# Moving the key half of the second memory projection from differential attention into the first mixing layer

## The chip, the cores and the metric

The kernel runs on one core of one Trainium2 chip. The metric is device microseconds from the first to the last instruction of one execution. TensorE is called PE, VectorE DVE, ScalarE ACT, GpSimd POOL, and SP is SyncE, the engine whose queue issues the loads.

## The reference

A block of two layers over 256 positions of width 1024, followed by a second block of two layers that the change doesn't touch. Each of the first block's layers mixes along the sequence (layer 0: an RWKV-7 recurrence on one half of the width and an S5 state space on the other; layer 1: differential attention), then attends to a memory of 256 rows, which is the same in both layers, then runs a feed-forward part (layer 1: 8 experts). Cut to what matters:

```python
for l in range(DEPTH):
    hn = rms_norm(h, norm_mix[l])
    if l % 2 == 0:
        z = hn @ hy_w_in[i]
        y_a = rwkv7_time_mix(z[..., :RWKV_COLS], ...)
        y_b = s5_ssm(z[..., RWKV_COLS:], ...)          # ends in a gelu and a gated product, the glu
        y_mix = jnp.concatenate([y_a, y_b], axis=-1) @ hy_w_out[i]
    else:
        y_mix = diff_attention(hn, da_w_qkv[i], ...)
    h = h + y_mix
    h = h + memory_cross_attention(rms_norm(h, norm_xattn[l]), rms_norm(mem, norm_mem[l]), ...)
    ...

def memory_cross_attention(h, mem_n, w_q, w_kv, q_gain, k_gain, w_o):
    k, v = jnp.split(mem_n @ w_kv, 2, axis=-1)
    k = rms_norm(k.reshape(b, m, MEM_HEADS, MEM_HEAD_DIM), k_gain)
    ...
```

Keys and values of the memory, `mem_n @ w_kv`, depend on nothing that a layer computes, so they can be made at any earlier time.

## The kernel before

All of it is one program, in stages one after the other: `mix0` (layer 0's mixing), `xa0` (its attention to the memory), `ff0`, `mix1` (differential attention), `xa1`, `ff1` (the experts), then the second block. Products run in a split form: a weight tile is loaded as `raw` (128x1024, 512 KB), ACT rounds it into `whi` (L270), DVE subtracts to get `wlo` (L271), and `mm3` issues three matmuls for each product (L320 to L322). `mix0` has 3 buffers of `raw` and 2 each of `whi` and `wlo`; the other stages have 6 of each.

`mem_kv(l)` is a generator that makes the memory's keys `kT` and values `v` of layer l. It loads the memory (two DMAs), normalizes and transposes it (`norm_T`: 16 transposes L385, 16 splits each on ACT L361 and on DVE L362, squares L401), then goes through four column groups c: 0 and 1 are the keys, 2 and 3 the values. A group is two weight tiles of two halves, with 12 matmuls of 512 columns to each half. A key group is then copied (kn, L548), its heads' squares are summed (L569), an rsqrt is made of them (L348 to L353), the heads are scaled (L519), transposed on PE (L522) and copied to `kT` (L524). A value group is only copied (L544).

Where this work stands in the program is set by hand: `drive(*gens, bg, slow, every)` steps through generators in turn, and each `yield` is a place where others may put their instructions. Each engine then takes its instructions in the order in which they were written, and waits on semaphores. In `mix0`, four recurrence units `mat(0..3)` are driven with the S5 part as `slow` and `mem_kv(0)` behind the rest of the input projections as `bg`; behind them come the glu (product with `yh`, `yl`, matmuls into `psB`) and the output projection. In `mix1`, `attn(0)` has the second half of the qkv projection as its background, `attn(1)` the whole of `mem_kv(1)`, in the order `KV_ORD[1]` = (0, 2, 1, 3); then follows `out_proj`. In `attn`, probabilities p are transposed (L734) and copied (`at`, L739), multiplied by the values (L741 to L743), the outputs copied (`on`, L749), squared (L751), reduced (L752), scaled by an rsqrt (L758), transposed (L761) and split into `oTh` and `oTl`.

Of the kernel before, what the change touches and what calls it, by code (L numbers as in the profile page):

```python
# [9 lines left out]
F32 = mybir.dt.float32  # L10
# [32 lines left out]
ZN = 2  # L43
EI = 2
SE = 2
SG = 1
# [158 lines left out]
def build(tc, dram, off, out, phases):  # L205
# [98 lines left out]
    def every_n(g, n):  # L304
        i = 0
        for _ in g:
            i += 1
            if i % n == 0:
                yield

    def idle(n):
        for _ in range(n):
            yield

    def chain(*fns):
        for f in fns:
            yield from f
# [177 lines left out]
            down_acc(y, lambda k: xh[:, k], lambda k: xl[:, k], name, i, order[0], -1)  # L495
        down_last(y, lambda k: xh[:, k], lambda k: xl[:, k], name, order[last:])

    mem_state, mem_pools, mem_ctx = {}, {}, {}

    def mem_kv(l, tag, st, xp=None):  # L500
        m = [wp.tile([128, 1024], F32, tag="raw", name="mem", bufs=nraw) for _ in range(2)] if rawc == 1024 else None
        if m is None:
            m2 = wp.tile([128, 2, 1024], F32, tag="raw", name="mem", bufs=nraw)
            m = [m2[:, t] for t in range(2)]
        for t in range(2):
            nc.sync.dma_start(m[t], dram("mem")[:, t])
        xh, xl, rm = norm_T(m, "norm_mem%d" % l, tag, xp)
        gk = ap.tile([128, 2], F32, tag="gk", name="gk", bufs=1)
        V.scalar_tensor_tensor(gk, colr("xa_q_gain%d" % l), 1.0 / 16.0, colr("xa_k_gain%d" % l),
                               op0=ALU.mult, op1=ALU.mult)  # L510
        p = mem_pools[l]
        kT, v = p.tile([128, 8, 256], F32, name="kT"), p.tile([128, 2, 1024], F32, name="v")
        mem_state[l] = (kT, v)
        yield
        def heads_T(c, kn, ks):
            for t in range(2):
                for a in range(2):
                    s = slice(a * 256, a * 256 + 256)
                    V.tensor_scalar(kn[t][:, s], kn[t][:, s], ks[t][:, a:a + 1], None, op0=ALU.mult)  # L519
                pt = psC((128, 4, 128))  # L520
                for b in range(4):
                    T.transpose(pt[:, b], kn[t][:, b * 128:(b + 1) * 128], ident)  # L522
                for b in range(2):
                    S.activation(kT[:, 4 * c + b:4 * c + 4:2, t * 128:t * 128 + 128], pt[:, b::2], AF.Copy,  # L524
                                 scale=gk[:, b:b + 1])

        pend = None
        for c in KV_ORD[l]:
            ps = [psA(tag=tag) for _ in range(2)]
            for j in range(2):  # L530
                w = wt("w_kv%d" % l, 2 * c + j)
                for kk in range(4):
                    k = 4 * j + kk
                    for t in range(2):
                        ts = slice(t * 128, t * 128 + 128)
                        wh, wl = w(kk * 512, 512)
                        mm3(ps[t], xh[:, k, ts], xl[:, k, ts], wh, wl, k == 0, k == 7)
                    yield
                if pend:
                    heads_T(*pend)  # L540
                    pend = None
            if c >= 2:
                for t in range(2):
                    S.activation(v[:, t, (c - 2) * 512:(c - 1) * 512], ps[t], AF.Copy, scale=rm[t])  # L544
                continue
            kn = [st.tile([128, 512], F32, tag="kn", name="kn", bufs=2) for _ in range(2)]
            for t in range(2):
                S.copy(kn[t], ps[t])  # L548
            pend = (c, kn, head_norm(kn, rm, 2, 256, st))
        if pend:  # L550
            heads_T(*pend)

    def open_kv(l):
        mem_ctx[l] = ExitStack()
        mem_pools[l] = mem_ctx[l].enter_context(
            tc.tile_pool(name="kv%d" % l, bufs=1, side="right", reuse_waits="tile"))

    def head_norm(src, rm, nh, d, st=None):
        ss = ap.tile([128, 2, nh], F32, tag="hn%d" % nh, name="hn", bufs=2)
# [14 lines left out]
        return [z[:, t] for t in range(2)]  # L574

    def xattn(l):
        kT, v = mem_state[l]
        xh, xl, rm = norm_T(ht, "norm_xattn%d" % l)
        oh = ap.tile([128, 8, 256], F32R, tag="oTh", name="oTh", bufs=1)
        ol = ap.tile([128, 8, 256], F32R, tag="oTl", name="oTl", bufs=1)  # L580
# [57 lines left out]
    def diff_attn():  # L638
# [135 lines left out]
            pass  # L774
        tags[0] = "D"
        pace = None
        open_kv(1)
        kv = mem_kv(1, "D", ap, ap)
        next(kv)
        bg = qkv(1)  # L780
        drive(paced(attn(0)), bg=every(bg, R0))
# [194 lines left out]
    def mix0():  # L976
        nonlocal junk_at
        with tc.tile_pool(name="z", bufs=1, reuse_waits="tile") as zp:
            rrow = zp.tile([128, 256], F32, name="rrow")
            yab = zp.tile([128, 8, 256], F32, tag="yab", name="yab", bufs=1)  # L980
            uT = zp.tile([128, 4, 256], F32, name="uT")
            def zpair(i):
                w = wt("w_z", i)
                for b in range(2):
                    n = ZB[2 * i + b]
                    if n == "Z":
                        continue
                    ps = psA((128, 256), "A")
                    for k in range(8):
                        mm3(ps, *w((b * 8 + k) * 128, 128), xh[:, k], xl[:, k], k == 0, k == 7)  # L990
                        if k == 3:
                            yield None
                    yield n, ps

            with tc.tile_pool(name="rw", bufs=1, reuse_waits="tile") as rp:
                open_kv(0)
                zx, s5x = ExitStack(), ExitStack()
                zxp = zx.enter_context(tc.tile_pool(name="zx", bufs=1, side="right", reuse_waits="tile"))
                junk_at = (zxp, 512)
                xh, xl, rm = norm_T(ht, "norm_mix0", xp=zxp)  # L1000
                bcast_row(rm, zp, rrow)
                with tc.tile_pool(name="s5prep", bufs=1, reuse_waits="tile") as sp:
                    s5c = s5_prep(zp, sp)

                def s5():
                    zx.close()
                    sp = s5x.enter_context(tc.tile_pool(name="s5", bufs=1, side="right", reuse_waits="tile"))
                    yield from s5_table(sp, s5c)
                    yield from s5_main(sp, s5c, yab, uT)

                rwkv(rp, zpair, yab, uT, rrow, s5())
                s5x.close()
            with tc.tile_pool(name="mo", bufs=1, reuse_waits="tile") as sp:
                junk_at = (sp, 512)
                s5_glu(sp, s5c, yab)
                mh = sp.tile([128, 8, 256], F32R, name="mh")
                ml = sp.tile([128, 8, 256], F32R, name="ml")
                for k in range(8):
                    split(mh[:, k], ml[:, k], yab[:, k])
                out_proj(mh, ml, "w_hyo", LM)  # L1020
                junk_at = None

    def rwkv(rp, zpair, ya, uT, rrow, s5g):
# [26 lines left out]
        def t2(name, shape, n=2):  # L1050
            return mp.tile(list(shape), F32, tag=name, name=name, bufs=n)
# [32 lines left out]
        zg = zgen()  # L1084
        nonlocal junk_at
        junk_at = (rp, 256)
        kv = mem_kv(0, "D", rp)
        mctx = ExitStack()

        def need(n):  # L1090
# [82 lines left out]
        def mat(p):  # L1173
# [47 lines left out]
            for j in range(5):  # L1221
# [17 lines left out]
                V.tensor_tensor(TN[:, lo:], TZ[:, lo:], pT[:, lo:], op=ALU.subtract)  # L1239
                TZ = TN  # L1240
                yield
            PQ = t2("PQ", (128, 4, 2, 64))
            pq = psB((128, 4, 128))
            heads(lambda c, g: T.matmul(pq[g, c], TZ[g, 1, c], X[g, c].rearrange("p a t -> p (a t)"), start=True, stop=True))
            S.mul(PQ.rearrange("p c a t -> p (c a t)"), pq.rearrange("p c t -> p (c t)"), -1.0)
            yield
            MT = t2("MT", (128, 4, 64))
            HT = t2("HT", (128, 4, 64))
            pm = psC((128, 4, 2, 64))
            heads(lambda c, g: T.matmul(pm[g, c, 0], PQ[g, c, 0], VB[g, c, 1], start=True, stop=True))  # L1250
# [23 lines left out]
            ms = t2("ms", (128, 8))  # L1274
            V.tensor_reduce(ms[:, :4], po, axis=AX, op=ALU.add)
            V.tensor_scalar(ms[:, :4], ms[:, :4], 1.0 / 64, None, op0=ALU.mult)
            ct = t2("ct", (128, 4, 64))
            V.tensor_tensor(ct, po, ms[:, :4, None].to_broadcast([128, 4, 64]), op=ALU.subtract)
            yield
            cq = e("cq", (128, 4, 64))  # L1280
# [24 lines left out]
        def zrest():  # L1305
            for _ in zg:
                yield
# [2 lines left out]
        drive(ew(0), ew(1))  # L1310
        next(kv)
        mp = mctx.enter_context(tc.tile_pool(name="mat", bufs=1, reuse_waits="tile"))
        drive(chain(mat(0), mat(2)), chain(idle(SG), mat(1), mat(3)), chain(ew(2), ew(3)),
              bg=chain(every_n(zrest(), ZN), kv), slow=slow, every=SE)
        drive(kv)
        drive(slow)
        mctx.close()

# [433 lines left out]
    for pi, ph in enumerate(phases):  # L1752
# [13 lines left out]
        with tc.tile_pool(name=ph, bufs=1, reuse_waits="tile") as ap:  # L1766
            if ph == "mix0":
                mix0()
            elif ph in ("xa0", "xa1"):
                l = int(ph[2])  # L1770
                if l not in mem_state:
                    open_kv(l)
                    drive(mem_kv(l, "D", ap, ap))
                xattn(l)
                mem_ctx[l].close()
            elif ph == "mix1":
                diff_attn()
            elif ph == "ff0":
                ffn(None)
            elif ph == "ff1":  # L1780
                moe()
                rq = None
            elif ph in ("b0", "b1"):
                block2(int(ph[1]))
            elif ph in ("bf0", "bf1"):
                ffn(int(ph[2]))
# [36 lines left out]
```

## Time and profile before

| | us |
|---|---|
| time, median of 3 runs (lowest, highest) | 2551.97 (2551.45, 2552.53) |
| the profiled execution: its span | 2550.7 |
| PE busy | 2437.5 (96%) |
| DVE busy | 2050.5 (80%) |
| ACT busy | 1501.3 (59%) |
| mean granted TensorE clock | 0.965 |

The profiled execution's own time is its span, 2550.7 us; the median of the timed runs lies 1.3 us above it. Busy shares are means over all stages; what a stage is limited by is read from stretches of it. A clock of 1.00 is 2.4 GHz and 0.50 is 1.2 GHz. In the timelines a row with a count stands for that many instructions one after the other, and a bracket gives the idle time before the row and the instruction that ended it.

### The profile page before, as it was taken

Reading aid. Unit: us, or ns where it says so; the run is one execution under the profiler, and the core shown is the slowest. Engines: PE = TensorE matmul, PEld = TensorE weight load, DVE = VectorE, ACT = ScalarE, POOL = GpSimd, SP = SyncE. Lnnn points to the kernel's source line nnn. Section 1 sums busy time; section 2 is a strip of 40 time slices with the busy share of each in tenths; the row PEclk is TensorE's granted clock in tenths of the full one; section 3 lists DMA queues with packets and bytes.
Section 4 is the critical chain, followed back from the end, with each engine's and each line's share of the span. In section 5 each row is a group of like instructions: output and inputs, shape, how many; then the busy total and the mean of one; then the engine's idle time right before and its main releaser. Section 6 shows DMA issues by size and latency. Waiting matters only on the chain. (4 is left out here: it accounts for less than half of the span.)

```text
span 2550.7 us, 38313 instructions
## 1 busy us (share of the span) xinstructions
PE 2437.5 (96%) x13843; PEld 2009.8 (79%) x13843; DVE 2050.5 (80%) x3526; ACT 1501.3 (59%) x2236; POOL 115.3 (5%) x144
## 2 busy tenths in 40 slices
PE   7979878999999989999999999999998999999999
PEld 6856657899777778787878787878786689976998
DVE  8696866666766569999999999998987778876886
ACT  6321225544656557777777777777775455564654
POOL 2341300000000000000000000000000000000000
PEclk9986979999999989999999999999998899998999
DMA  5310115455534559999998999999994355552553
GB/s 183 103 43 25 51 58 189 157 184 188 169 108 141 190 178 373 357 330 356 357 357 324 362 357 326 361 326 366 348 356 152 100 167 189 184 182 76 185 186 107
DMA packets 154756, 558.12 MB, mean 219 GB/s; under 512 B 17568, under 2 KB 18208, under 8 KB 154560
## 3 DMA queue, kind: packets, MB, share of 16 engines
q1 hardware_dynamic: 152064, 551.62, 61.2%
q10 hardware_dynamic: 2496, 3.99, 0.5%
q8 instruction: 110, 1.80, 0.3%
q14 instruction: 86, 0.70, 0.1%
HBM read 554.50 MB, written 1.05 MB: 218 GB/s over the span
## 5 line engine op out<-in xcount | busy, mean ns | idle before, releaser
L271 DVE TENSOR_TENSOR wlo<-raw,whi 128x1024 fp32r<-128x1024 f32 x1044 | 1254.2, 1227 | 208.9 <-ACT whi L270 195.8
L270 ACT CAST whi<-raw 128x1024 fp32r<-128x1024 f32 x1044 | 1074.6, 1050 | 553.6 <-PE psA L322 249.2
L321 PE MATMUL psB<-wlo,xeh 128*128 128x512 f32 x880 | 351.3, 399 | 3.3 <-DVE wlo L271 3.3
L322 PE MATMUL psB<-whi,xel 128*128 128x512 f32 x880 | 348.0, 395 | 0.0
L320 PE MATMUL psB<-whi,xeh 128*128 128x512 f32 x880 | 345.4, 396 | 0.1
L321 PE MATMUL psB<-xTl,whi 128*128 128x256 f32 x1008 | 283.7, 282 | 0.0
L320 PE MATMUL psB<-xTh,whi 128*128 128x256 f32 x1008 | 281.8, 283 | 1.5 <-DVE fg L1734 1.5
L322 PE MATMUL psB<-xTh,wlo 128*128 128x256 f32 x1008 | 282.4, 281 | 0.0
L321 PEld LDWEIGHTS psB<-wlo,xeh 128*128 128x128 f32 x880 | 165.2, 188 | 48.0 <-DVE wlo L271 9.6
L320 PEld LDWEIGHTS psB<-whi,xeh 128*128 128x128 f32 x880 | 165.3, 188 | 39.8 <-ACT whi L270 1.0
L322 PEld LDWEIGHTS psB<-whi,xel 128*128 128x128 f32 x880 | 165.3, 188 | 37.8
L322 PEld LDWEIGHTS psB<-xTh,wlo 128*128 128x128 f32 x1008 | 191.0, 190 | 0.4
L321 PEld LDWEIGHTS psB<-xTl,whi 128*128 128x128 f32 x1008 | 189.6, 188 | 1.1
L320 PEld LDWEIGHTS psB<-xTh,whi 128*128 128x128 f32 x1008 | 187.5, 187 | 3.2 <-DVE fg L1734 2.1
L320 PE MATMUL psA<-whi,xTh 128*128 128x512 f32 x416 | 171.8, 421 | 4.8 <-ACT whi L270 4.6
L321 PE MATMUL psA<-wlo,mhh 128*128 128x512 f32 x448 | 175.8, 394 | 0.2
L322 PE MATMUL psA<-whi,mhl 128*128 128x512 f32 x448 | 173.9, 392 | 1.2 <-DVE mhl L359 1.2
L321 PE MATMUL psA<-wlo,xTh 128*128 128x512 f32 x416 | 169.9, 412 | 0.5 <-DVE wlo L271 0.5
L322 PE MATMUL psA<-whi,xTl 128*128 128x512 f32 x416 | 164.1, 409 | 0.0
L320 PE MATMUL psA<-whi,mhh 128*128 128x512 f32 x448 | 152.5, 392 | 1.7 <-ACT mhh L358 1.7
L320 PE MATMUL psA<-whi,hh 128*128 128x512 f32 x264 | 103.3, 391 | 1.5 <-ACT hh L358 1.5
L321 PE MATMUL psA<-wlo,hh 128*128 128x512 f32 x264 | 103.2, 391 | 0.0
(570 smaller groups left out, 3882.3 us busy)
## 6 DMA issues: line engine op xcount, KB each, us to landing
raw<-in_w_moe SPq DMA_DIRECT2D x672, 512.0 KB, 6.1
raw<-in_w_bfu SPq DMA_DIRECT2D x88, 512.0 KB, 4.2
raw<-in_w_ffu SPq DMA_DIRECT2D x44, 512.0 KB, 4.5
raw<-in_w_bfd SPq DMA_DIRECT2D x44, 512.0 KB, 4.1
raw<-in_w_kv SPq DMA_DIRECT2D x32, 512.0 KB, 3.6
raw<-in_w_in SPq DMA_DIRECT2D x32, 512.0 KB, 5.4
raw<-in_w_qkv SPq DMA_DIRECT2D x24, 512.0 KB, 4.5
raw<-in_w_ffd SPq DMA_DIRECT2D x22, 512.0 KB, 4.5
```

Source lines behind the costliest of these rows:

```text
L270: S.copy(hi, raw[:, r])
L271: V.tensor_tensor(lo, raw[:, r], hi.bitcast(F32), op=ALU.subtract)
L320: T.matmul(ps, ah, bh, start=st, stop=False)
L321: T.matmul(ps, ah, bl, start=False, stop=False)
L322: T.matmul(ps, al, bh, start=False, stop=sp)
```

## The change

The keys of layer 1 are made in `mix0`, behind those of layer 0: `mem_kv` takes an `order` of column groups, and `chain(mem_kv(0), mem_kv(1, order=(0, 1)))` is the background of the recurrence. What is left of the background when the recurrence units are done is written out by `drive(bg)`. In `mix1`, `mem_kv(1)` runs with groups (2, 3) alone; it loads and normalizes the memory as it did, so the normalization for layer 1 is done in both places. The pool of keys and values of a layer is opened in two parts, and the keys' part for layer 1 lives from `mix0` on. To make room, `PQ` shares the buffers of `TZ`, `MT` those of `Y` and `ct` those of `HT` in the recurrence units.

```diff
-    def mem_kv(l, tag, st, xp=None):
+    def mem_kv(l, tag, st, xp=None, order=None):
+        order = order or KV_ORD[l]
...
-        p = mem_pools[l]
-        kT, v = p.tile([128, 8, 256], F32, name="kT"), p.tile([128, 2, 1024], F32, name="v")
-        mem_state[l] = (kT, v)
+        kT, v = mem_state.get((l, "k")), mem_state.get((l, "v"))
...
-        for c in KV_ORD[l]:
+        for c in order:
...
-    def open_kv(l):
-        mem_ctx[l] = ExitStack()
-        mem_pools[l] = mem_ctx[l].enter_context(
-            tc.tile_pool(name="kv%d" % l, bufs=1, side="right", reuse_waits="tile"))
+    def open_kv(l, part):
+        mem_ctx.setdefault(l, ExitStack())
+        p = mem_ctx[l].enter_context(
+            tc.tile_pool(name="kv%d%s" % (l, part), bufs=1, side="right", reuse_waits="tile"))
+        mem_state[l, part] = p.tile([128, 8, 256] if part == "k" else [128, 2, 1024], F32, name="kT" if part == "k" else "v")
...
-        open_kv(1)
-        kv = mem_kv(1, "D", ap, ap)
+        open_kv(1, "v")
+        kv = mem_kv(1, "D", ap, ap, (2, 3))
...
-                open_kv(0)
+                open_kv(1, "k")
+                open_kv(0, "k")
+                open_kv(0, "v")
...
-        kv = mem_kv(0, "D", rp)
+        kv = chain(mem_kv(0, "D", rp), mem_kv(1, "D", rp, order=(0, 1)))
...
-            PQ = t2("PQ", (128, 4, 2, 64))
+            PQ = t2("TZ", (128, 4, 2, 64), 4)
...
-            MT = t2("MT", (128, 4, 64))
+            MT = t2("Y", (128, 4, 64))
...
-            ct = t2("ct", (128, 4, 64))
+            ct = t2("HT", (128, 4, 64))
...
-        drive(chain(mat(0), mat(2)), chain(idle(SG), mat(1), mat(3)), chain(ew(2), ew(3)),
-              bg=chain(every_n(zrest(), ZN), kv), slow=slow, every=SE)
-        drive(kv)
+        bg = chain(every_n(zrest(), ZN), kv)
+        drive(chain(mat(0), mat(2)), chain(idle(SG), mat(1), mat(3)), chain(ew(2), ew(3)), bg=bg, slow=slow, every=SE)
+        drive(bg)
         drive(slow)
```

What this does to the order of instructions is shown at three places. Lines of the changed kernel are a few lower or higher than those of before (L521 there is L522 here, L1297 and L1298 are L1295 and L1296).

First, PE at the end of `mix0`: `zG` and `gu` are the last recurrence unit's gate, `yh` and `yl` the glu's input. Before:

```order
L1107 MATMUL psC<-ident,ct 64x64
L1110 MATMUL psC<-rwc,ct 64x64 x2
L1295 MATMUL psC<-zG_475,gu_396 128x256
L1296 MATMUL psC<-zG_1471,gu_398 128x256
L320 MATMUL psB<-yh,whi 128x256 x2
L321 MATMUL psB<-yl,whi 128x256
```

After, with the gate at the top and 66 matmuls from L320 to L322 from the first of them to the last ahead of L521, of which the inner ones are left out:

```order
L1297 MATMUL psC<-zG_484,gu_405 128x256
L1298 MATMUL psC<-zG_1478,gu_407 128x256
L320 MATMUL psA<-whi,xTh 128x512
L321 MATMUL psA<-wlo,xTh 128x512
...
L322 MATMUL psA<-whi,xTl 128x512
L521 MATMUL psC<-ident,kn 128x128 x16
L320 MATMUL psB<-yh,whi 128x256 x2
L321 MATMUL psB<-yl,whi 128x256
```

Between the last gate and the glu there now stand 66 of the 96 key matmuls and all 16 transposes of key heads; the other 30 stand among the last steps of the recurrence.

Second, ACT at the same place: `ln` is the recurrence unit's last norm, `yh` the glu's input. Before:

```order
L1518 ACTIVATE y_3246<-y_3246 128x256
L1290 ACTIVATE ln<-psC,cols 128x256
L1281 ACTIVATE cq<-ct 128x256
L1290 ACTIVATE ln<-psC,cols 128x256
L358 CAST yh<-yab 128x1024
```

After, from the first key group's squares on (the last `ln` stands six rows higher):

```order
L569 ACTIVATE hj,hn<-kn 128x256 x3
L270 CAST whi<-raw 128x1024 x4
L523 ACTIVATE kT<-psC,gk 128x2x128 x2
L547 COPY kn<-psA 128x512
L523 ACTIVATE kT<-psC,gk 128x2x128 x2
L547 COPY kn<-psA 128x512
L569 ACTIVATE hj,hn<-kn 128x256 x4
L523 ACTIVATE kT<-psC,gk 128x2x128 x4
L358 CAST yh<-yab 128x1024
```

The copies, squares and `kT` of both key groups moved in ahead of the cast that makes the glu's input.

Third, DVE in `mix1`, from the rsqrt behind the last output reduction to the multiplication that uses it and the split of the output. Before (rows of another rsqrt, that of the key heads, lie between):

```order
L336 SCALAR_TENSOR_TENSOR rs_y<-rs_t,rs_y 128x4
L336 SCALAR_TENSOR_TENSOR rs_y<-rs_t,rs_y 128x8
L334 TENSOR_TENSOR rs_t<-rs_x,rs_y 128x4
L758 TENSOR_TENSOR on<-on,rs_y 128x512 x2
L335 TENSOR_TENSOR rs_t<-rs_t,rs_y 128x4
L271 TENSOR_TENSOR wlo<-raw,whi 128x1024
```

After:

```order
L334 TENSOR_TENSOR rs_t<-rs_x,rs_y 128x8
L271 TENSOR_TENSOR wlo<-raw,whi 128x1024
L335 TENSOR_TENSOR rs_t<-rs_t,rs_y 128x8
L271 TENSOR_TENSOR wlo<-raw,whi 128x1024
L336 SCALAR_TENSOR_TENSOR rs_y<-rs_t,rs_y 128x8
L271 TENSOR_TENSOR wlo<-raw,whi 128x1024
L758 TENSOR_TENSOR on<-on,rs_y 128x512 x2
L271 TENSOR_TENSOR wlo<-raw,whi 128x1024
L362 SCALAR_TENSOR_TENSOR oTl<-psC,dgs,oTh 128x4x128 x2
```

Three `wlo` now stand inside the rsqrt ahead of L758, and a fourth ahead of `oTl`. On PE, between the last products with the values and the transposes L761, 24 background matmuls stand where 54 stood, and between the last L734 and those products 2 where 20 stood.

## Rows read from the trace of the kernel before

**Rows 1.** The page: span, busy times, one row of the DMA issues

```profile
span 2550.7 us, 38313 instructions
...
PE 2437.5 (96%) x13843; PEld 2009.8 (79%) x13843; DVE 2050.5 (80%) x3526; ACT 1501.3 (59%) x2236; POOL 115.3 (5%) x144
...
raw<-in_w_kv SPq DMA_DIRECT2D x32, 512.0 KB, 3.6
```

**Rows 2.** Stretches of the second mixing layer; behind POOL: clock, DMA share, GB/s

```profile
800.00:810.00 10.00, 9.86 (x53) 8.22 (x52) 6.32 (x15) 8.77 (x21) 0.00 (x0) 1.00 0.64 211
810.00:820.00 10.00, 10.00 (x48) 8.16 (x48) 9.28 (x30) 6.75 (x8) 0.00 (x0) 1.00 0.43 141
```

**Rows 3.** Stretches at the end of the first mixing layer: PE, PEld, DVE, ACT, POOL, clock

```profile
310.00:320.00 10.00, 8.83 (x97) 5.66 (x92) 8.93 (x17) 2.31 (x3) 5.11 (x5) 1.00 0.14 46
320.00:330.00 10.00, 4.72 (x71) 3.40 (x70) 9.93 (x31) 0.42 (x1) 3.66 (x5) 0.76 0.10 37
330.00:340.00 10.00, 6.30 (x22) 2.83 (x20) 5.87 (x20) 1.63 (x4) 1.66 (x2) 0.50 0.00 1
340.00:350.00 10.00, 7.02 (x22) 3.68 (x21) 4.52 (x21) 2.32 (x6) 0.00 (x0) 0.50 0.01 2
```

**Rows 4.** Timeline of PE in the second mixing layer

```profile
799.03 0.40 PE L320 MATMUL psA<-whi,xTh 128*128 128x512 f32 x1
...
801.60 0.40 PE L322 MATMUL psA<-whi,xTl 128*128 128x512 f32 x1
801.83 1.04 PE L522 MATMUL psC<-ident,kn 128*128 128x128 f32 x8
802.71 0.39 PE L741 MATMUL psA<-dv,at 128*128 128x128 f32 x2
```

**Rows 5.** Timeline of DVE behind the last products with the values

```profile
807.05 1.28 DVE L752 TENSOR_REDUCE oss<-hj 128x4 f32<-128x512 f32 x2 [2.70 <-ACT hj L751]
...
811.35 1.29 DVE L758 TENSOR_TENSOR on<-on,rs_y 128x512 f32<-128x512 f32 x2
```

**Rows 6.** Timeline of ACT in the same place

```profile
802.99 0.83 ACT L524 ACTIVATE kT<-psC,gk 128x256 f32<-128x256 f32 x2
803.71 0.58 ACT L548 COPY kn<-psA 128x512 f32<-128x512 f32 x1
...
805.37 1.11 ACT L749 COPY on<-psA 128x512 f32<-128x512 f32 x2
...
807.77 0.42 ACT L569 ACTIVATE hj<-kn 128x256 f32<-128x256 f32 x1 [0.23 <-DVE oss L752]
...
809.58 0.19 ACT L569 ACTIVATION_READ_ACCUMULATOR hj<-kn 128x1 f32 x1
```

**Rows 7.** Groups of instructions by line and form, 700 to 840

```profile
L271 DVE TENSOR_TENSOR wlo<-raw,whi 128x1024 fp32r<-128x1024 f32 x34 | 41.5, 1224 | 22.7 <-ACT whi L270 22.3
L270 ACT CAST whi<-raw 128x1024 fp32r<-128x1024 f32 x34 | 35.7, 1051 | 26.0 <-PE psA L322 26.0
```

**Rows 8.** Groups of instructions by line and form, 30 to 60

```profile
L362 DVE SCALAR_TENSOR_TENSOR xTl<-psA,cols,xTh 128x128 fp32r<-128x128 f32 x10 | 3.4, 346 | 0.0
```

**Rows 9.** Timeline of DVE in the first mixing layer: a head norm of layer 0's keys

```profile
221.48 0.16 DVE L348 TENSOR_TENSOR rs_in<-hn,r 128x4 f32<-128x4 f32 x1
...
224.32 0.16 DVE L353 TENSOR_TENSOR rf<-rs_y 128x4 f32<-128x4 f32 x1
```

**Rows 10.** Timeline of PE at the end of the first mixing layer

```profile
344.36 0.34 PE L1106 MATMUL psC<-rwc,ct 64*128 64x64 f32 x1 [2.91 <-DVE ct L1284]
...
347.99 1.22 PE L1296 MATMUL psC<-zG,gu 32*128 32x256 f32 x2
349.14 0.80 PE L320 MATMUL psB<-yh,whi 128*128 128x256 f32 x2
```

**Rows 11.** Groups of instructions by line and form, 210 to 350

```profile
L519 DVE TENSOR_SCALAR kn<-kn,rf 128x256 f32<-128x256 f32 x4 | 1.6, 468 | 0.0
```

**Rows 12.** Timeline of ACT at the end of the first mixing layer

```profile
347.42 1.03 ACT L358 CAST yh<-yab 128x1024 fp32r<-128x1024 f32 x1
```

More of the change, by code (lines that the diff above doesn't have):

```diff
@@ L496, in out_proj @@
         down_last(y, lambda k: xh[:, k], lambda k: xl[:, k], name, order[last:])
-    mem_state, mem_pools, mem_ctx = {}, {}, {}
-    def mem_kv(l, tag, st, xp=None):
+    mem_state, mem_ctx = {}, {}
+    def mem_kv(l, tag, st, xp=None, order=None):
+        order = order or KV_ORD[l]
         m = [wp.tile([128, 1024], F32, tag="raw", name="mem", bufs=nraw) for _ in range(2)] if rawc == 1024 else None
@@ L576, in xattn @@
     def xattn(l):
-        kT, v = mem_state[l]
+        kT, v = mem_state[l, "k"], mem_state[l, "v"]
         xh, xl, rm = norm_T(ht, "norm_xattn%d" % l)
@@ L1770, in build @@
                 l = int(ph[2])
-                if l not in mem_state:
-                    open_kv(l)
+                if (l, "k") not in mem_state:
+                    open_kv(l, "k")
+                    open_kv(l, "v")
                     drive(mem_kv(l, "D", ap, ap))
```

## The prediction

> **What bounds the kernel now.** I read the page first. TensorE (PE) is busy 96% of the span [rows 1], so most of the kernel is a stream of matmuls, and the question is whether PE is the limit in the two stages that the change touches. The table by stretches answers it. In the second mixing layer PE is busy 9.86 to 10.00 us of every 10, at a granted clock of 1.00 (2.4 GHz), while VectorE (DVE) and ScalarE (ACT) have room [rows 2]. Work taken from PE there is time gained, as long as what is left still covers the attention's chain on ACT and DVE. At the end of the first mixing layer it is the other way round: DVE is busy 8.93 and 9.93 of 10 us until 330, PE 8.83 and 4.72, and from 330 to 350 PE is busy 6.30 and 7.02 us at a clock of 0.50 (1.2 GHz), which is 3 to 3.5 us of work at full speed [rows 3]. There PE waits for a chain (rsqrt, transposes, gates), not for its own work. So the change moves work from a stage that has no idle PE into one that has some. Where in that stage the matmuls land decides.
>
> **The units.** In the timeline of PE, 11 steps of 512-column matmuls lie between 799.03 and 801.60: 0.234 us each; the 8 transposes of key heads take 802.71 - 801.83 = 0.88 us, 0.11 each [rows 4]. The Trainium skill, "TensorE: Matmul & The Clock Gate", section "Back-to-back issue gap", gives a sustained 131 ns for N=512. The row shows 1.8 times that; by the page's figure 96 matmuls would be an estimated 12.6 us instead of 22.4, and 66 of them 8.6 instead of 15.4. The measured spacing decides and is what I use.
>
> **What the second mixing layer gains.** The key half reads 8 pieces of `w_kv1` of 128x1024, with 12 matmuls to each: 96 of the 192 matmuls that ran behind attn(1), and 16 transposes with them. 96 x 0.234 = 22.4, 16 x 0.11 = 1.8: 24.2 us of PE time leave a stretch in which PE never idles. Its ACT and DVE work (8 head squares, 4 copies, 8 scalings, the second rsqrt chain) leaves too, off the limit.
>
> The cover gets thinner. In before, by the order, 54 background matmuls stand between the last products with the values (L741 to L743) and the transposes of the output (L761): 12.6 us in which the chain runs unseen. It is a copy of `on` on ACT from 805.37, squares, a reduction on DVE to 808.33, an rsqrt and the multiplication L758 from 811.35 [rows 5, 6]. In after, the order leaves 24 there (5.6 us), and three `wlo` subtractions have moved into the rsqrt chain ahead of L758. Start of the copy to start of L758 took 811.35 - 805.37 = 5.98 us; the chain of the other head_norm that shared DVE there is gone (-0.4), three `wlo` at 1.22 [rows 7] add 3.7, and the first half of L758 takes 0.65: 9.9 us from the copy to the first transpose. Covered: 5.6, and 0.75 of the copy itself, for which the 24 matmuls must wait since they need its PSUM buffers. PE idles about 0.75 + 3.6 there, about 1.2 behind the transposes (a fourth `wlo` stands between L758 and oTl, and the 36 matmuls behind need oTh and oTl), and 0.4 at the `at` copies, before which two matmuls are left instead of 20: 6 us given back. Bounds: nothing, if `wlo` falls earlier than the order lets me think, to 9 (another 1.22 us and a late weight). **Gain 18, between 15 and 24.**
>
> **What the first mixing layer pays.** Up to about 298 us the orders of PE, DVE, ACT and SyncE are the same, so I expect the traces alike to there. The tile sharing (PQ with TZ, MT with Y, ct with HT) lies on buffers whose readers are long done by the order: nothing, and the cover is the time between the last reader and the next writer; without it every one of the four recurrence units would show new waits before 298.
>
> (a) *The end of the recurrence is pushed.* The memory is normalized for the second layer in this stage: 16 transposes, 8 squares on ACT, 16 splits each on ACT and DVE (DVE 0.346 each [rows 8]: 5.5 us), some 17 small DVE operations (0.16 each [rows 9]: 2.7) and two more `wlo` (2.4) stand ahead of the last gate: 10.6 us of DVE, in a stretch where DVE is busy 9 to 10 of 10 until 330 and half free after it [rows 3]. 30 of the 96 matmuls and the transposes also lie ahead of that gate, in PE's idle time. I take two thirds: **+7, between -6 and +10** (-6: the clock, see the first rival).
>
> (b) *66 matmuls stand behind the last gate and ahead of the glu.* In before, the glu's first matmul starts 1.15 us after the last gate's [rows 10]. In after, `drive(bg)` writes out the rest of the key half there: 66 x 0.234 = 15.4 us at full clock. PE comes into it from half clock, and each 12 matmuls need a `whi` (1.05) and then a `wlo` (1.22) [rows 7], in buffers of which this stage has two: 2.3 us of preparation under 2.8 of matmuls, which hides unless the head-norm chain on DVE stands between. I add 2.6 for both. **+18, between 15.4 and 22.**
>
> (c) *Then PE idles for the key's own tail.* The 16 transposes L521 stand between the last key matmul and the glu, and ACT's order puts kT x2, kn, kT x2, kn, four squares, kT x4 ahead of `yh<-yab`, which the glu reads. From rows: first four transposes 0.5; a pair of kT (0.83) and a kn (0.58), twice, less 0.4 that overlaps: 2.4; four squares 807.77 to 809.77: 2.0; the head-norm chain L348 to L353, 221.48 to 224.48: 3.0; scaling, first two of four at 0.47 each: 0.9; transposes 0.6; the last pair of kT 0.83; `yh` 1.03 [rows 4, 6, 9, 11, 12]. Sum 11.3; take **+11.5, between 9.5 and 13**. In before, `yh` (from 347.42 [rows 12]) was made beside the last gate's matmuls; nothing but these steps stands on PE in that time. The glu's weights land long before and stay hidden, and the queue of SyncE is 8 weight loads and the two of the memory longer here and 8 shorter later; with 512 KB landing in 3.6 us [rows 1] that is no limit in either place.
>
> **The sum.** 7 + 18 + 11.5 - 18 = +18.5. The profiled execution of before spans 2550.7 us [rows 1], 1.3 under the median of its runs, 2551.97. Span after 2569.2, time **2570**. Later stages run the same instructions and only start later. A measurement of this kernel can tell about 0.2%, 5.1 us, from no change.
>
> **Rivals.**
>
> *Faster: the tail is free because the clock stays up.* From 330 to 350 PE runs at half clock in before [rows 3], and the chain's transposes and gates (344.36 to 349.14, 4.8 us [rows 10]) wait on it. 30 matmuls and 16 transposes put into this stretch could hold the clock at 1.00: half of the 13.3 us that PE is busy in these 20 comes back, about 6, and hides what (a) adds. With (b) and (c) at their floors and the whole gain: -6 + 15.4 + 9.5 - 24.2 = -5.3, time 2546.7. It decides where the glu's first matmul comes less than the second layer's gain later than 349.14. For it: PE idles there. Against it: DVE, not PE, is full until 330, and 66 of 96 matmuls lie behind everything. The Trainium skill, same page, Part 1 on the clock gate, has the gate follow how busy PE has been lately, which speaks for a part of this rival; the granted clock of 0.50 where PE has gaps and of 1.00 where it has none agrees.
>
> *No change: the two cancel.* (a) hides in DVE's half-free time after 330 (0), (b) at its floor of 15.4, (c) at 9.5 since part of kT lies beside the matmuls, gain 22 to 24: +1 to +3, time 2553 to 2555. Against it: (b) and (c) are in the order of the instructions, so they need no luck. PE could avoid them only by taking the glu first; the Trainium skill, same page, "Step-by-step: what each phase is for", says that matmuls stay in program order and only weight loads are taken ahead.
>
> *Much slower: the gain is mostly eaten.* The chain to L761 lies wholly bare because the weights of the second layer's `wlo` come late (SyncE's order has them behind the memory's loads), gain 12; the 66 matmuls run one half after the other behind DVE's queue (22); +10 and 13: +33, time 2585.
>
> **How the numbers follow.** Slower as in the sum, with the terms inside their bounds (+6 to +28): 0.76. Much slower: 0.08. No change: 0.09. Faster: 0.07. The predicted time is that of the sum. From below 0.07 and part of the 0.09 are left out, from above most of the 0.08: 2556 to 2582. The likeliest case's own range is 2558 to 2580.
>
> **What would show it.** In the trace of after: the glu's first matmul (psB<-yh,whi) 34 to 40 us later than 349.14, near 386; ahead of it 66 psA<-whi,xTh kinds, then 16 psC<-ident,kn with some 10 us of idle PE around them whose releasers are ACT (kT, kn) and DVE (kn, rf). From the first matmul of the second mixing layer to the first of the following cross-attention 16 to 20 us less; a wait of PE for `on` at L761, of 3 to 4 us, which before does not have. Step (a) is wrong if the last gate stands at 348 +- 1; (b) if the 66 take clearly more than 18; (c) if the idle time ahead of the glu is under 8. The prediction as a whole is wrong if the glu comes less than 25 us later, or if the second layer gives back nothing of its 24.

## The result, and the profile after

The changed kernel takes 2568.89 us (median of 4 runs, 2567.36 to 2571.69) against 2552.25 for before on the same chip: a ratio of 1.0062, 95% interval 1.0048 to 1.0077, or 16.6 us more; the interval lies above 1, so it is slower, by less than 1%. Forecast were 2570 us and slower. The page of the profiled execution, to set beside [rows 1]:

```profile
span 2568.1 us, 38423 instructions
...
PE 2439.3 (95%) x13859; PEld 2011.3 (78%) x13859; DVE 2056.2 (80%) x3558; ACT 1511.1 (59%) x2268; POOL 114.4 (4%) x144
```

PE is busy 1.8 us longer (2437.5 before): the matmuls were moved, not saved, and 15.6 of the 17.4 us of longer span are time in which PE waits. The last row in which a stage adds to the residual `h` (L484) marks the stage's end. Before, at the ends of the first mixing layer, the first feed-forward part and the second mixing layer:

```profile
384.42 0.69 DVE L484 TENSOR_TENSOR h<-psA,h 128x512 f32<-128x512 f32 x1 [0.51 <-PE psA L322]
...
652.03 0.68 DVE L484 TENSOR_TENSOR h<-psA,h 128x512 f32<-128x512 f32 x1
...
841.40 0.69 DVE L484 TENSOR_TENSOR h<-psA,h 128x512 f32<-128x512 f32 x1 [0.63 <-PE psA L322]
```

After:

```profile
424.58 0.69 DVE L484 TENSOR_TENSOR h<-psA,h 128x512 f32<-128x512 f32 x1 [0.50 <-PE psA L322]
...
693.16 0.68 DVE L484 TENSOR_TENSOR h<-psA,h 128x512 f32<-128x512 f32 x1
...
862.70 0.69 DVE L484 TENSOR_TENSOR h<-psA,h 128x512 f32<-128x512 f32 x1 [0.47 <-PE psA L322]
```

The first mixing layer ends 40.2 us later, the second takes (862.70 - 693.16) = 169.5 us in place of 189.4, 19.8 less, and all other stages together 3 less. Where the 40 come from is seen in PE's timeline at the end of the first layer, the counterpart of [rows 10]:

```profile
355.68 0.79 PE L320 MATMUL psA<-whi,xTh 128*128 128x512 f32 x1
...
358.40 1.05 PE L1297 MATMUL psC<-zG,gu 128*128 128x256 f32 x2
359.39 1.22 PE L1298 MATMUL psC<-zG,gu 32*128 32x256 f32 x2
360.54 0.80 PE L320 MATMUL psA<-whi,xTh 128*128 128x512 f32 x1
...
364.08 0.40 PE L322 MATMUL psA<-whi,xTl 128*128 128x512 f32 x1
...
377.89 1.03 PE L521 MATMUL psC<-ident,kn 128*128 128x128 f32 x8
386.97 1.94 PE L521 MATMUL psC<-ident,kn 128*128 128x128 f32 x8 [8.05 <-DVE kn L518]
390.77 0.80 PE L320 MATMUL psB<-yh,whi 128*128 128x256 f32 x2 [1.86 <-ACT yh L358]
```

The last gate starts 11.4 us later than in before (359.39 against 347.99), the 66 key matmuls take 377.89 - 360.54 = 17.35, and from their end to the glu's first matmul 12.9 us pass. Together the glu comes 41.6 us later. The waits of PE in this stretch (columns: total us, times, longest us):

```profile
PE psC L521 <- DVE kn L518: 8.0, 1, 8.0
PE psA L320 <- DVE xTl L362: 5.8, 1, 5.8
PE psC L1108 <- DVE HT L1286: 4.6, 1, 4.6
PE psB L320 <- ACT yh L358: 1.9, 1, 1.9
```

The second row is new with the memory's normalization: PE stands before the first key matmul, at 335.74, until DVE has made the split `xTl` that it reads. The third has its like in before (`ct`, [rows 10]). The first and the fourth are the key's own tail. On ACT it reads

```profile
378.09 1.05 ACT L270 CAST whi<-raw 128x1024 fp32r<-128x1024 f32 x1 [1.75 <-PE psA L322]
379.04 0.83 ACT L523 ACTIVATE kT<-psC,gk 128x256 f32<-128x256 f32 x2
...
381.42 0.46 ACT L569 ACTIVATE hj<-kn 128x256 f32<-128x256 f32 x1
...
388.10 1.69 ACT L523 ACTIVATE kT<-psC,gk 128x256 f32<-128x256 f32 x4 [4.50 <-PE psC L521]
389.68 1.04 ACT L358 CAST yh<-yab 128x1024 fp32r<-128x1024 f32 x1
```

and on DVE

```profile
383.63 0.16 DVE L348 TENSOR_TENSOR rs_in<-hn,r 128x4 f32<-128x4 f32 x1 [3.23 <-ACT hj L569]
...
386.20 0.16 DVE L353 TENSOR_TENSOR rf<-rs_y 128x4 f32<-128x4 f32 x1
```

kT and kn, squares, rsqrt, scaling, transposes, kT and only then the glu's `yh`, one behind the other. By stretches (columns as in [rows 3]):

```profile
320.00:330.00 10.00, 8.46 (x104) 6.24 (x103) 9.64 (x31) 3.09 (x9) 1.88 (x3) 0.82 0.26 74
330.00:340.00 10.00, 4.26 (x10) 2.93 (x11) 9.61 (x31) 2.46 (x7) 4.02 (x4) 0.50 0.26 86
340.00:350.00 10.00, 8.62 (x40) 5.15 (x40) 5.21 (x14) 3.59 (x6) 0.00 (x0) 0.99 0.15 52
350.00:360.00 10.00, 6.80 (x23) 4.67 (x23) 3.14 (x15) 0.56 (x1) 0.00 (x0) 0.52 0.16 52
...
380.00:390.00 10.00, 1.94 (x8) 1.57 (x8) 3.94 (x21) 5.39 (x17) 0.00 (x0) 0.55 0.20 69
```

DVE is now full to 340 where it was full to 330. The clock stands at half in 330 to 340 and nearly so in 350 to 360, but at 0.99 in 340 to 350, where before had 0.50 [rows 3]. From 380 to 390 no engine is busy for more than 5.4 of 10 us: a chain, not a load.

In the second mixing layer the wait foretold at L761 is there, with the three `wlo` ahead of L758 (timeline of DVE; then the wait of PE):

```profile
839.23 1.28 DVE L752 TENSOR_REDUCE oss<-hj 128x4 f32<-128x512 f32 x2 [6.35 <-ACT hj L751]
...
843.11 1.23 DVE L271 TENSOR_TENSOR wlo<-raw,whi 128x1024 fp32r<-128x1024 f32 x1 [0.58 <-ACT whi L270]
844.33 1.22 DVE L271 TENSOR_TENSOR wlo<-raw,whi 128x1024 fp32r<-128x1024 f32 x1
845.55 1.22 DVE L271 TENSOR_TENSOR wlo<-raw,whi 128x1024 fp32r<-128x1024 f32 x1
846.68 1.28 DVE L758 TENSOR_TENSOR on<-on,rs_y 128x512 f32<-128x512 f32 x2
```

```profile
PE psC L761 <- DVE on L758: 3.3, 1, 3.3
```

### The profile page after: what moved, and what is told of

Read it like the earlier page. It is cut to its first block, busy times and chain, and to the rows that moved or that the text cites. A ratio compares the mean times of both kernels' runs of the same rounds, so it can differ in the third digit from the quotient of the medians.

```text
span 2568.1 us, 38423 instructions
## 1 busy us (share of the span) xinstructions
PE 2439.3 (95%) x13859; PEld 2011.3 (78%) x13859; DVE 2056.2 (80%) x3558; ACT 1511.1 (59%) x2268; POOL 114.4 (4%) x144
## 5 line engine op out<-in xcount | busy, mean ns | idle before, releaser
L322 PE MATMUL psB<-whi,xel 128*128 128x512 f32 x880 | 348.0, 395 | 0.0
L320 PE MATMUL psB<-whi,xeh 128*128 128x512 f32 x880 | 345.5, 396 | 0.1
L320 PE MATMUL psB<-xTh,whi 128*128 128x256 f32 x1008 | 281.7, 283 | 1.5 <-DVE fg L1736 1.5
L322 PE MATMUL psB<-xTh,wlo 128*128 128x256 f32 x1008 | 282.5, 281 | 0.0
L320 PEld LDWEIGHTS psB<-whi,xeh 128*128 128x128 f32 x880 | 165.2, 188 | 39.9 <-ACT whi L270 1.0
L322 PEld LDWEIGHTS psB<-whi,xel 128*128 128x128 f32 x880 | 165.3, 188 | 38.0
L322 PEld LDWEIGHTS psB<-xTh,wlo 128*128 128x128 f32 x1008 | 190.9, 189 | 0.4
L320 PEld LDWEIGHTS psB<-xTh,whi 128*128 128x128 f32 x1008 | 187.7, 188 | 3.2 <-DVE fg L1736 2.1
L320 PE MATMUL psA<-whi,xTh 128*128 128x512 f32 x416 | 173.7, 427 | 10.5 <-DVE xTl L362 5.8
L322 PE MATMUL psA<-whi,mhl 128*128 128x512 f32 x448 | 173.9, 392 | 1.2 <-DVE mhl L359 1.2
L321 PE MATMUL psA<-wlo,xTh 128*128 128x512 f32 x416 | 171.7, 416 | 1.4 <-DVE wlo L271 1.3
L322 PE MATMUL psA<-whi,xTl 128*128 128x512 f32 x416 | 165.1, 413 | 0.0
L320 PE MATMUL psA<-whi,mhh 128*128 128x512 f32 x448 | 152.4, 392 | 1.7 <-ACT mhh L358 1.7
L320 PEld LDWEIGHTS psA<-whi,xTh 128*128 128x128 f32 x416 | 81.7, 197 | 35.2 <-DVE xTl L362 6.2
L320 PE MATMUL psA<-whi,hh 128*128 128x512 f32 x264 | 103.4, 392 | 1.5 <-ACT hh L358 1.5
```

Source lines behind the costliest of these rows:

```text
L320: T.matmul(ps, ah, bh, start=st, stop=False)
L321: T.matmul(ps, ah, bl, start=False, stop=False)
L322: T.matmul(ps, al, bh, start=False, stop=sp)
```

## The experiments

My theory: the first layer pays about 36 us in three parts (the recurrence pushed by DVE work, the 66 matmuls, the key's tail), and the second gains 18. Rivals: the tile sharing has a share in it; the gain or the cost is another one and the sum right by chance; PE, not DVE, is what the recurrence has no room on. Each group of experiments has its own runs of before: 2550.37 us (e1 to e4), 2550.78 (e5 to e8) and 2550.90 (e9 to e12).

**e1, the tile sharing alone.**

```diff
-        kv = chain(mem_kv(0, "D", rp), mem_kv(1, "D", rp, order=(0, 1)))
+        kv = mem_kv(0, "D", rp)
...
-        kv = mem_kv(1, "D", ap, ap, (2, 3))
+        kv = mem_kv(1, "D", ap, ap)
```

> The changed kernel with the key half left in the second mixing layer: the tile sharing, the split pools and the new drive calls alone. If the sharing costs nothing (my step), the time is that of before, 2552 within 5 us, and the last gate of the recurrence starts at 348 +- 1. If the sharing of PQ, MT and ct makes the recurrence wait (rival: it is a part of the 11.4 us by which the last gate came later), the last gate comes at 351 or later and the time is 2555 to 2563.

2549.42 us, ratio 0.9999 (0.9989 to 1.0008). The last gate starts at 346.88. The sharing costs nothing; that rival falls.

**e2, no key half at all** (the first edit of e1, and `G.memset(mem_state[1, "k"], 0.01)` ahead of `mem_kv(1, ..., (2, 3))`).

> The key half is in neither place; the keys of the second layer are a constant that POOL writes in the second mixing layer, so 96 matmuls, 16 transposes and what feeds them are left out. This shows what the second mixing layer gains by itself. By the traces the stage ends 19.8 us earlier against its start in the changed kernel: 2532 +- 3. If the gain were the whole 24.2 us of PE time, with nothing given back to the attention's chain, 2528. If the three us of difference between the stage and the end of the span are part of the change (later stages run faster), 2529.

2534.67 us, ratio 0.9929 (0.9909 to 0.9949): 15.7 us under before by the medians, 18.1 by the ratio. The second mixing layer is 18.2 us shorter in its profile, with the same wait of 3.3 us at L761. The gain stands near 18, and the full 24.2 would need 2526.

**e3, the key's tail late**: for the second key group, squares, rsqrt and scaling behind the casts of the output projection's input, transposes and kT behind the projection.

```diff
+            if late:
+                hold += [late_norm, late_T]
+                return
             pend = (c, kn, head_norm(kn, rm, 2, 256, st))
...
+                hold[0](sp)
                 out_proj(mh, ml, "w_hyo", LM)
+                hold[1]()
```

> The changed kernel, with the second key group's squares, rsqrt and scaling written behind the casts of the output projection's input and its 8 transposes and kT behind the output projection. The 66 matmuls stay where they are. If the 12.9 us between the last key matmul and the glu are the key's own tail on ACT and DVE (my step c), about 9 to 10 of them go: kT, kn and yh stay ahead of the glu, some 3.5 us. Time 2559 +- 3, the glu at 381. If the idle time is the glu's own (its yh waits for something else, weights or buffers), the time stays at 2569.

2569.50 us, ratio 1.0077 (1.0059 to 1.0095): the step in the trace is as expected, the time isn't. The glu starts at 379.13, 4.2 us behind the last key matmul in place of 12.9. But the 8 transposes now stand bare at the head of the cross-attention,

```profile
419.19 1.12 PE L565 MATMUL psC<-ident,kT 128*128 128x128 f32 x4 [1.38 <-DVE xTl L362]
421.10 1.11 PE L565 MATMUL psC<-ident,kT 128*128 128x128 f32 x4 [0.79 <-DVE xTl L362]
```

and against e5's profile the first layer is 8.0 us shorter, the cross-attention behind it 4.6 longer, the second mixing layer 2.6 longer and the rest 1.0 longer. e6 takes the transposes out of the cross-attention.

**e4, two steps of memory work a round.**

```diff
-        bg = chain(every_n(zrest(), ZN), kv)
+        bg = chain(every_n(zrest(), ZN), every(kv, 2))
...
-        drive(bg)
+        drive(kv)
```

> The changed kernel, with two steps of the memory work for each round of the recurrence in place of one, so that all of the key half stands ahead of the last gate and nothing between that gate and the glu. If the position behind the gate is what costs (steps b and c, 30 us), and DVE takes the rest: the recurrence ends 10 to 25 us later than in before, since the key half adds some 26 us of DVE work to a stage in which DVE is busy three quarters of the time, and the second layer gains 20: 2542 to 2557. If PE's idle time in the recurrence could take it for nothing (the rival with no cost in the first layer), 2532 to 2538. If DVE or the buffers of whi and wlo hold the recurrence up as much as the tail did, 2565 or more.

2567.99 us, ratio 1.0062 (1.0044 to 1.0079). No key matmul stands between the last gate and the glu any more, and the glu is no earlier for it:

```profile
346.88 1.94 PE L521 MATMUL psC<-ident,kn 128*128 128x128 f32 x8 [6.86 <-DVE kn L518]
...
382.96 1.22 PE L1298 MATMUL psC<-zG,gu 32*128 32x256 f32 x2
384.11 0.80 PE L320 MATMUL psB<-yh,whi 128*128 128x256 f32 x2
```

The recurrence itself ends 35.0 us later than in before (382.96 against 347.99). It was the third case of the expectation: the stage has no room for this work in either of the two places. e7 and e8 ask on which engine.

**e5 and e11, the changed kernel again**, each beside the others of its group.

> The changed kernel unaltered, on the same chip as the three that follow, so that they are compared with it and not only with before: +16 to +18 against before.

> The changed kernel beside the one above: +16 to +19 against before. If the stage lengths behind the first layer depend on when the stage begins, the second mixing layer may take another time than the 169.6 us of its two profiles though the instructions are the same.

2568.95 us, ratio 1.0071 (1.0049 to 1.0092), and 2569.53, 1.0072 (1.0058 to 1.0086): +18.2 and +18.6 against before. The last gate stands at 356.99 and 358.93. The 12.9 us of the tail and the 169.5 to 169.6 us of the second mixing layer are the same in all three profiles.

**e6 and e10, the tail beside the glu**: as e3, with `hold[0](sp)` ahead of the glu's matmuls and `hold[1]()` behind them.

> As the late tail, but with the second key group's squares, rsqrt and scaling beside the glu's matmuls and its 8 transposes and kT between the glu and the output projection, where the late tail had put them into the start of the cross-attention. If step (c) is real and the late tail lost its gain only because it stood bare again further on, the output projection ends about 10 us earlier than in the changed kernel, and nothing is given back: 9 to 11 us faster than the changed kernel. If the tail merely moves to whatever stands next (rival), the two are within 3 us.

> The kernel with the tail at the glu once more, in more rounds beside the changed kernel: its first layer ended 10.8 us earlier in the profile, but the median was only 0.7 us lower. If the gain is there and the runs merely scatter, 5 to 10 us under the changed kernel. If it is given back behind the first layer (in its profile the second mixing layer took 174.7 us against 169.6, with a lower granted clock in part of it), 0 to 4 us under it.

2568.26 and 2566.62 us, 0.7 and 2.9 under the changed kernel of the same group, where 9 to 11 were expected if nothing is given back; as times they are what the rival foretold. In e10's profile the glu stands 22.7 us behind the last gate, in e11's 31.4; in e6's 20.7, in e5's 31.4. So 8.7 to 10.7 are gained there, and step (c) is real. About 5 are given back: the second mixing layer takes 174.5 and 174.7 us in the two profiles of this kernel, 169.5 to 169.6 in the three of the changed one. (The rest of e10's gain is mostly a last gate that stands 2.5 us later than e11's; e6's profile is of its fastest execution, 2561.89 us.)

That stage has the same instructions in all five profiles, but not in the same order. In the changed kernel, 17 background matmuls stand on PE between two groups of score products (L713, L714); in e6 and e10 the same products (L737, L738) follow one another, and the background comes behind them. The edit adds and takes nothing in this stage, and no run shows why its order came out another way. The changed kernel, then e6:

```profile
741.66 0.70 PE L714 MATMUL psB<-dqT 64*128 64x256 f32 x2
742.28 0.50 PE L320 MATMUL psA<-whi,xTh 128*128 128x512 f32 x1
...
747.89 0.28 PE L713 MATMUL psB<-dr,si 128*128 128x256 f32 x1
```

```profile
728.29 1.22 PE L738 MATMUL psB<-dqT 64*128 64x256 f32 x2
729.44 0.58 PE L737 MATMUL psB<-dr,si 128*128 128x256 f32 x1
...
732.76 0.79 PE L320 MATMUL psA<-whi,xTh 128*128 128x512 f32 x1
```

The granted clock differs too (the first figure behind the last bracket, as in [rows 2]). The whole stage in before (with the key half), in the changed kernel, in e3 and in e6:

```profile
652.03:841.40 189.37, 184.57 (x839) 143.25 (x838) 126.41 (x333) 113.74 (x240) 1.27 (x1) 0.96 0.44 146
```

```profile
693.16:862.70 169.54, 159.75 (x727) 122.63 (x727) 111.53 (x284) 96.40 (x203) 1.55 (x1) 0.97 0.42 136
```

```profile
687.34:859.52 172.18, 163.64 (x727) 125.60 (x727) 111.67 (x284) 96.72 (x203) 1.18 (x1) 0.94 0.39 134
```

```profile
679.41:854.11 174.70, 166.66 (x727) 127.44 (x727) 112.07 (x285) 96.90 (x203) 1.18 (x1) 0.92 0.39 132
```

PE is busy 6.9 us longer in e6 than in the changed kernel with the same 727 records. Both profiles have a place where DVE is full, PE has gaps and the clock is below 1.00; in e6 it then stands at 0.50 for 5 us in which PE is full. First the changed kernel, then e6:

```profile
730.00:735.00 5.00, 2.74 (x11) 1.84 (x12) 5.00 (x21) 2.46 (x7) 0.00 (x0) 0.77 0.57 195
```

```profile
717.00:722.00 5.00, 3.72 (x14) 2.72 (x15) 4.96 (x19) 3.20 (x9) 0.00 (x0) 0.57 0.45 154
...
732.00:737.00 5.00, 5.00 (x12) 3.48 (x12) 2.39 (x6) 1.02 (x4) 0.00 (x0) 0.50 0.00 0
```

Over all profiles without the key half in this stage its length goes with its clock: 169.5 to 169.6 us at 0.97 (the changed kernel, three times), 171.2 and 171.7 at 0.95 (e2, e4), 172.2 and 172.5 at 0.94 (e3, e7), 174.5 to 174.7 at 0.92 (e6, e8, e10). e3 and e4 have the order of the changed kernel here, so some 2 to 2.6 us come without a change of order. How much of the 5 in e6 and e10 is the other order's, and whether the first layer's earlier end has a part in it, was not tried.

**e7, e4 with one matmul of three** in the key's products.

```diff
+                        if order == (0, 1):
+                            T.matmul(ps[t], xh[:, k, ts], wh, start=k == 0, stop=k == 7)
+                        else:
+                            mm3(ps[t], xh[:, k, ts], xl[:, k, ts], wh, wl, k == 0, k == 7)
```

> The kernel with two steps a round, with only one of the three matmuls of each product of the second memory's keys (the two with the rounding remainders are left out): 32 matmuls of 512 columns in place of 96, with all of the ACT and DVE work. If PE is what the recurrence has no room on, 64 x 0.234 = 15 us or more go, since part of them ran at half clock: the last gate comes 15 to 25 us earlier than 383. If DVE is what has no room, it moves by less than 5 us.

2568.24 us, ratio 1.0059 (1.0042 to 1.0077), no faster than e4; the last gate at 379.09, 3.9 us earlier than in e4. That is within the scatter: in seven other profiles with the same order up to the last gate (the changed kernel, e3, e5, e6, e10, e11, e12) it stands anywhere from 355.55 to 362.50. So 64 matmuls fewer are worth nothing that shows. Two rows of stretches say why; e4's comes first. What is left in e7 stands partly in another order, so they are not quite the same place of the program:

```profile
300.00:320.00 20.00, 18.08 (x112) 12.65 (x110) 18.98 (x40) 7.66 (x16) 6.14 (x5) 1.00 0.40 141
```

```profile
300.00:320.00 20.00, 7.96 (x29) 3.79 (x27) 19.80 (x50) 5.88 (x14) 5.64 (x6) 0.66 0.40 131
```

DVE is as full as it was (19.80 of 20), PE idles more, and its granted clock is 0.66 there in place of 1.00. The Trainium skill, "TensorE: Matmul & The Clock Gate", Part 1 on the clock gate, says that the gate goes by how busy PE has been; these two rows (18.08 and 7.96 us of 20) agree. Most of that idle time is one wait for DVE, in e7's timeline of PE:

```profile
316.54 1.06 PE L1514 MATMUL psA<-R,s5c 128*32 128x256 f32 x2 [10.84 <-DVE R L1511]
```

**e8, e4 without remainders**: `lo = hi` for the second memory's key weights and its normalized rows.

> The kernel with two steps a round, with all 96 matmuls of the second memory's keys, but without their remainders: the 8 wlo and the 16 xTl are left out, and the matmuls read the rounded values in their place. DVE loses 8 x 1.22 + 16 x 0.35 = 15.4 us, PE nothing. If DVE has no room, the last gate comes 12 to 16 us earlier than 383; if PE has none, less than 5.

2561.24 us, ratio 1.0041 (1.0028 to 1.0054), 6.8 under e4's median and 7.0 under e7's of the same group; the last gate at 374.84, 8.1 us earlier than in e4, a little more than the scatter. That is neither case of the expectation (12 to 16, or under 5): DVE's work counts where PE's doesn't show, but for about half of its 15.4 us.

**e9, the second normalization alone** (`order=()` in the first layer, keys and values both in the second).

> The changed kernel with only the second memory's load, squares, transposes and splits moved into the first mixing layer (they are done again in the second, with keys and values both there), and no key matmul moved. This is the part of step (a) that is not matmuls: 16 xTl (5.5 us) and some small operations on DVE, 16 transposes on PE. If DVE is what the end of the recurrence has no room on, the last gate comes 4 to 8 us later than 347 to 348 and the time is 2555 to 2559; if what pushed the gate in the changed kernel were the blocks of six matmuls ahead of it, less than 2 us, and 2551 to 2553.

2557.25 us, ratio 1.0025 (1.0016 to 1.0034): +6.3 us, so the normalization alone costs time. Where it does is less sure. The last gate stands at 352.16, 4.2 us later than in before and 5.3 later than in e1; but e2's, with the order of before up to there, stands at 352.63. And in e9's profile the second mixing layer takes 192.2 us in place of 189.4, with its instructions in another order there too. That the normalization is 4 to 5 of the 9 to 11.4 us of step (a) is an estimate from single profiles.

**e12, the key half in both places** (`mem_kv(1, "D", ap, ap)` in the second layer).

> The key half made in both places, first as in the changed kernel and again in the second mixing layer: the cost in the first layer without the gain in the second. By the first layer's traces +38 to +40 against before, 2588 to 2591; by the medians (the changed kernel less the kernel without any key half, 2569 - 2535) +34, 2585. If the two places influence one another, something else.

2586.60 us, ratio 1.0134 (1.0119 to 1.0150): the first layer's cost by itself is 35.7 us. With e2's 15.7 that makes +20.0; by the ratios it is 34.2 less 18.1, +16.1. The changed kernel measured +16.6 to +18.6, so the two places add up within the scatter.

## Why the prediction was right

The direction and the size hold, and the mechanism with them: the cost of the first layer, the gain of the second and the harmless sharing each have a run of their own (e12, e2, e1). Of the terms inside the cost, (c) is shown by e3, e6 and e10, (a) in part by e9, and (b) is read from the trace. That the sum comes within 1.1 us of the span's 17.4 is partly luck: by the profile the glu comes 5.1 us later than the 36.5 forecast, and against that stand 1.4 that come back before the stage's end, 1.8 more gain and 2.9 in the other stages.

- **Cost of the first layer, 36.5 forecast:** 35.7 by e12. In the trace the glu is 41.6 us later, just beyond the 34 to 40 that I gave; the layer's end 40.2, and part of the rest comes back in the stages behind.
- **(a), +7:** 11.4 in the first profile, 9.0 and 10.9 in the other two, near or above the upper bound of 10; in e3, e6, e10 and e12, with the same order up to the gate, 7.6 to 14.5. The scatter of the gate in before has to be added: 346.88 to 352.63 in before, e1 and e2. Mis-sized: I took two thirds of the DVE work, and left out that six key matmuls stand at half clock ahead of the last gate (355.68 to 358.40, 2.7 us), where I had counted them into PE's idle time. What these six are worth has no run of its own.
- **(b), +18:** 17.35, or 1.9 above full clock. Nearly all of that is the start at half clock: the first eight matmuls take 364.08 - 360.54 = 3.5 us, where 0.234 each make 1.9. No wait for a `wlo` shows on PE in this stretch.
- **(c), +11.5:** 12.9, the same in three profiles. The chain is the one worked out; above its 11.3 come a cast of `whi` that holds the first kT until 379.04, and a last row of four kT in 1.69 us where a pair of 0.83 was counted. It is a true cost of the stage's end (8.7 to 10.7 us go when it is moved), but of the whole time only 0.7 to 2.9 went with it.
- **Gain of the second layer, 18:** 19.8 in the profile, 15.7 to 18.1 by e2. PE is busy 24.8 us less in this stage (159.75 in place of 184.57; 24.2 were worked out) and idles 5.0 more (6 were). The chain of the attention's output was bared as the order said, with 3.3 us at L761 where 3.6 were worked out. Two readings behind this term were weak: the stage was read from 20 of its 189 us, in one of which stretches DVE was busy 9.28 of 10 and had little room [rows 2], and the sum has no term for the clock, which over the runs lies between 0.97 and 0.92 in this stage, with 169.5 to 174.7 us.
- **Later stages, unchanged:** 3 us less in the profile. Most of that lies behind the cross-attention, where before's profile took 1634.8 us, and those of e1 and e2 1631.4 and 1631.5 with the same instructions: scatter, as far as these show, not the change.

Of the rivals, "faster" fell at its own point: the glu came 41.6 us later, more than the second layer's gain. Its mechanism is there for 10 us only: with the 30 matmuls and 16 transposes the clock stands at 0.99 in 340 to 350, but at 0.50 and 0.52 in the stretches before and after. The forecast's own range, +6 to +28, was a judgement: the bounds of its terms add up to about -5 to +30. "No change" fell with (a), (b) and (c), "much slower" with the gain. What stays open: e4 ends the recurrence 35 us later with everything spread over it; taking out two thirds of PE's share returns 3.9 of that, taking out 15.4 us of DVE's share 8.1, each in one profile. The two were not taken out together, and ACT's share not at all. That the rest is in the order of dependent steps behind one another is a guess that no run tests.

## What to carry to other kernels

Moving work out of a stage whose bound engine hardly idles was worth its time on that engine here (24.8 us), less what it was covering (5.0): look for the chain that ran behind it. Moving it into a stage with idle time on that engine was not free, because the idle time was a chain on another engine that the moved work loads too: the 24 us of PE work brought 22 us of DVE work with it (DVE is busy 312.4 us up to the first layer's end in place of 290.3). And when a background is drained behind the last foreground step, its own tail (norm, transposes, copies) stands bare and has to be priced as a chain.

## What the runs showed of the hardware

The second mixing layer without the key half took 169.5 to 174.7 us in ten profiles, in step with a mean granted clock of 0.97 to 0.92 over the stage. In five of these the order of its instructions is the same, and it took 169.5 to 172.2 us at 0.97 to 0.94. A gain ahead of such a stage can vanish in it, as 5 of 9 to 11 us did in e6 and e10, where the order had changed as well. And taking 64 matmuls out of a stretch where PE already waits went with a lower clock for those left (0.66 in place of 1.00 in 300 to 320) and saved nothing in the time. Runs of one kernel scatter by more than I took for granted: before ran from 2546.15 to 2556.95 us over the groups, and the glu started at 349.14, 348.03 and 353.78 in three profiles (before, e1, e2) whose order of instructions is the same up to there. In e2's the clock is already at 0.84 in 310 to 320 and at 0.50 in 320 to 330, where before has 1.00 and 0.76 [rows 3]; what sets that off was not tried.
